# 32 bytes between the 128-feature chunks of the normed tokens and of the FFN's inner tiles

## The chip, the core and the metric

The kernel runs on one core of a Trainium2 chip. The metric is device time in microseconds for one execution of the whole program, the median of several runs. Lower is better.

## What is computed

256 tokens of 1024 features go through two transformer layers and then a third block. Each of the two layers is an FFN, an attention mixer with 16 heads, and another FFN; the third block has a recurrent mixer beside a latent attention, then a layer of 16,384 experts that are found by key products, and a last gated projection. Cut to the parts that the change touches:

```
def rms_norm(x, g):
    y = xf * lax.rsqrt(jnp.mean(xf * xf, axis=-1, keepdims=True) + RMS_EPS)
    return y * g

def swiglu(x, w_gate, w_up, w_down):
    return (jax.nn.silu(x @ w_gate) * (x @ w_up)) @ w_down

for layer in range(DEPTH):
    x = x + 0.5 * swiglu(rms_norm(x, norm_ffn1[layer]), ...)
    x = x + mixed(rms_norm(x, norm_mix[layer]) @ w_in ...) @ w_out[layer]
    x = x + 0.5 * swiglu(rms_norm(x, norm_ffn2[layer]), ...)
...
h = rmsnorm(x, g_mix);  u = h @ w_in              # 4384 columns
x = x + merged @ w_out
x = x + peer_ffn(rmsnorm(x, g_ffn), ...)          # gelu(h @ expert_u.T), gates, @ expert_v
x = x + (p @ w_ple_proj) * sigmoid(rmsnorm(x, g_ple) @ w_ple_gate)
```

All inputs are float32, and D_FF is 2816.

## The kernel before

Activations lie feature-major: a tile of 128 partitions has one chunk of 256 tokens for each 128 features, so `x`, `xnh` and `xnl` have KD = 8 chunks and the FFN's inner tiles `hh` and `hl` have KF = 22. A chunk is 256 float32 values, 1024 bytes of each partition.

Precision comes from splitting. Every value is kept as a high part in float32r and the rest in a second float32r tile (`xnh` and `xnl` for the normed tokens, `hh` and `hl` for the inner activations, `o0` and `o1` for the gated expert activations, `gh` and `gl` for the tokens of the key products, `yh` and `yl` for the mixers' outputs). A product takes three matmuls: high by high, low by high, high by low.

Nearly all work is streaming weights once. `wblk` (line 186) loads a block of four 128x128 weight tiles, 256 KB, by a DMA on SP's queue into `wr`, ScalarE makes the high part `wh` (line 195), and VectorE or GpSimd, as the stage says, makes the rest `wl` (line 201). Each of `wr`, `wh` and `wl` has 2048 bytes a partition and comes from the pool `wp` with four buffers, or, for every fifth block, from a second pool with one.

`ws` (line 213) then runs three matmuls for each of the four weight tiles, with the weights as the stationary operand and a 256-column chunk as the moving one:

```
self.nc.tensor.matmul(out, wh[:, s], h, start=first, stop=False, **kw)   # line 224
self.nc.tensor.matmul(out, wh[:, s], l, start=False, stop=False, **kw)   # line 225
self.nc.tensor.matmul(out, wl[:, s], h, start=False, stop=last, **kw)    # line 226
```

So a product with 8 chunks is two blocks and 24 matmuls. The stages, in order, are:

- `ffn` (line 282), four times: 22 x 2 products with `xnh` and `xnl` for gate and up, then 8 products of 22 chunks with `hh` and `hl` for down.
- `mix`, after the first FFN of each layer: 2 x 16 products with `xnh` and `xnl` as moving operand for queries and keys, 8 chunks x 2 x 2 x 3 matmuls for the values, where the tokens are the stationary operand and 512 weight columns move (lines 205 to 207), attention, and the output product with `yh` and `yl`. In the second layer `forget_gates` runs the same `xnh` and `xnl` chunks against weights of 8 columns (lines 159, 205 to 207).
- `mix2`: 35 products with `xnh` and `xnl`, the recurrence and the latent attention among them; `xnh` and `xnl` then hold other values for 96 and 192 more matmuls.
- `peer`: the key products with `gh` and `gl`, then 128 calls of `u_phase` (line 1237), one product with `xnh` and `xnl` each. 30 of them run while the key products' top 16 are sorted, with `wl` made by GpSimd; 34 in a loop that VectorE feeds with one-hot tiles (lines 1266 to 1285); 64 in turn with the first 64 of 128 calls of `v_phase` (line 1290), which stream `o0` and `o1` (lines 1302 to 1304).
- `ple`: the last gate, 8 products with `xnh` and `xnl`.

Tiles are placed in SBUF pool by pool, in the order in which they are made. Bytes from the partition's start, as the built program has them: `xnh` at 10,496 and `xnl` at 18,688, then the weight tiles from 26,880 on (`wh` of the first buffer at 35,072), `hh` at 65,824 and `hl` at 88,352, `o0`, `o1`, `gh`, `gl`, `yh` and `yl` behind 65,536. Every 128x128 weight tile starts at 256 modulo 512, whichever buffer it is in. Every chunk of `xnh` and `xnl` starts at 256, too; every chunk of `hh`, `hl`, `yh` and `yl` at 288, and of `o0`, `o1`, `gh` and `gl` at 320. "Offset" below is the start of the moving chunk less that of the weight tile, modulo 512: 0 for `xnh` and `xnl`, 32 for `hh`, `hl`, `yh` and `yl`, 64 for the others.

Of the kernel before, what the change touches and what calls it, by code (L numbers as in the profile page):

```python
# [10 lines left out]
F32R = mybir.dt.float32r  # L11
# [9 lines left out]
T = 256  # L21
D = 1024
KD = D // 128
FF = 2816
KF = FF // 128
# [117 lines left out]
class Prog:  # L143
    def __init__(self, ctx, tc, A):
        self.ctx, self.tc, self.nc, self.A = ctx, tc, tc.nc, A
        nc = self.nc
        self.const = ctx.enter_context(tc.tile_pool(name="const", bufs=1))
        self.table("natural_log_exp_and_others")
        self.vec = self.const.tile([128, N_VEC], F32, name="vec")
        nc.sync.dma_start(self.vec, A["vec"])  # L150
        self.ones = self.const.tile([128, 128], F32, name="ones")
        nc.vector.memset(self.ones, 1.0)
        self.eps = self.const.tile([128, 1], F32, name="eps")
        nc.vector.memset(self.eps, 1e-6)
        self.x = self.const.tile([128, KD, T], F32, name="x")
        self.xnh = self.const.tile([128, KD, T], F32R, name="xnh")
        self.xnl = self.const.tile([128, KD, T], F32R, name="xnl")

    def col(self, name, i=0):
        o, n = VEC_COLS[name]  # L160
# [121 lines left out]
    def ffn(self, gname, gu, dn, also=None):  # L282
        nc, tc = self.nc, self.tc
        self.norm(gname)
        with tc.tile_pool(name="hp", bufs=1) as hp:
            hh = hp.tile([128, KF, T], F32R, name="hh")
            hl = hp.tile([128, KF, T], F32R, name="hl")
            for f in range(KF):
                if f == 4 and also is not None:
                    also()  # L290
                p = self.pair("mm")
                for j in range(2):
                    self.ws(p[:, j], gu[f, j], self.xnh, self.xnl, KD)
                if f == 0:
                    self.norm_factor()
                s = self.tmp.tile([128, 2, T], F32, name="s")
                nc.vector.tensor_mul(s, p, self.rs2())
                nc.scalar.activation(s[:, 0], s[:, 0], AF.Silu)
                nc.vector.tensor_mul(s[:, 0], s[:, 0], s[:, 1])
                self.split(hh[:, f], hl[:, f], s[:, 0])  # L300
            for d in range(KD):
                p = self.pair("mm")
                self.ws(p[:, 0], dn[d], hh, hl, KF)
                nc.vector.scalar_tensor_tensor(self.x[:, d], p[:, 0], 0.5, self.x[:, d], op0=ALU.mult, op1=ALU.add)
# [1235 lines left out]
```

## Time and profile before

| | |
|---|---|
| median of 3 runs | 2279.07 us (2274.92 to 2279.41) |
| the profiled execution | 2276.94 us |
| its span | 2275.2 us |
| TensorE, matmuls | 2196.3 us busy, 97%, 18034 matmuls |
| TensorE, weight loads | 2114.0 us busy, 93% |
| VectorE | 1617.6 us, 71% |
| ScalarE | 1346.1 us, 59% |
| GpSimd | 283.0 us, 12% |
| HBM, mean over the span | 159 GB/s read and written |

The profiled execution lies 1.7 us above its own span, which is what stands before the first and after the last instruction, and 2.1 us under the median of the runs. Busy time is the union of an engine's records. Matmuls overlap in the records, so their mean duration is longer than the time from one to the next. Stages can be told by the tiles: a window of the trace in which only `xnh` and `xnl` are streamed is a gate and up projection, one with `hh` and `hl` a down projection.

### The profile page before, as it was taken

What the parts mean: (1) busy time and instruction counts of PE and PEld (TensorE: products, weight loads), DVE (VectorE), ACT (ScalarE), POOL (GpSimd) and SP (SyncE); (2) the same over time, 40 slices, a digit from 0 to 9 for tenths busy, and PEclk for the clock granted to TensorE, in tenths of its full rate; (3) what the DMA queues carried; (4) which work ended last, traced back from release to release, by engine and by line L of the source; (5) the groups of instructions that cost most, each with busy time, mean ns of one, the idle gap of its engine ahead of it and who ended that gap; (6) DMA issues with size and microseconds to landing.
All of it is one profiled execution on the core that took longest, in us unless ns stands there. A gap on an engine that the chain in (4) does not pass through costs nothing.

```text
span 2275.2 us, 48212 instructions
## 1 busy us (share of the span) xinstructions
PE 2196.3 (97%) x18034; PEld 2114.0 (93%) x18034; DVE 1617.6 (71%) x3293; ACT 1346.1 (59%) x2667; POOL 283.0 (12%) x272
## 2 busy tenths in 40 slices
PE   8999999999999999999888989889999999999997
PEld 8999889999999789999787889889999999999997
DVE  7766777666766757766886577999996666666666
ACT  6555576556555556556765656456665555555556
POOL 1001100000000101001233027960000000000001
PEclk9999999999999999999998999999999999999999
DMA  6566425565567325565243145443346555555553
GB/s 208 183 181 193 125 94 192 183 183 187 184 179 223 116 83 173 183 181 185 86 134 113 47 156 172 149 140 112 121 144 206 185 185 186 183 189 189 187 186 117
DMA packets 209659, 365.30 MB, mean 161 GB/s; under 512 B 31056, under 2 KB 39312, under 8 KB 208912
## 3 DMA queue, kind: packets, MB, share of 16 engines
q1 hardware_dynamic: 207312, 361.96, 50.4%
q8 instruction: 141, 2.31, 0.4%
q14 instruction: 94, 0.77, 0.1%
q10 hardware_dynamic: 2112, 0.26, 0.1%
HBM read 357.87 MB, written 4.26 MB: 159 GB/s over the span
## 4 chain that ended last, share of the span: by engine, by line
PE 82%; DVE 9%; ACT 3%; DMA 2%; POOL 2%; issue 2%; SPq 0%; DVEq 0%; POOLq 0%; ACTq 0%
PE mm L224 13%; PE mm L226 13%; PE mm L225 13%; PE acc L1302 5%; PE acc L1304 5%; PE acc L1303 5%; PE pu L225 5%; PE pu L224 5%; PE pu L226 5%; DVE wl L201 2%; PE pg L1282 2%; POOL wl L201 1%; DMA wr<-in_pu 1%; PE w L347 1%; PE mm L205 1%
## 5 line engine op out<-in xcount | busy, mean ns | idle before, releaser
L195 ACT ACTIVATE wh<-wr 128x512 fp32r<-128x512 f32 (+1 forms) x1348 | 836.4, 624 | 697.0 <-PE mm L225 240.5
L201 DVE TENSOR_TENSOR wl<-wr,wh 128x512 fp32r<-128x512 f32 (+1 forms) x1234 | 851.6, 696 | 485.5 <-ACT wh L195 455.7
L224 PE MATMUL mm<-xnh,wh 128*128 128x256 f32 x1840 | 529.2, 288 | 10.6 <-ACT wh L195 7.3
L226 PE MATMUL mm<-xnh,wl 128*128 128x256 f32 x1840 | 524.4, 285 | 1.6 <-POOL wl L201 0.9
L225 PE MATMUL mm<-xnl,wh 128*128 128x256 f32 x1808 | 514.7, 285 | 0.1
L224 PEld LDWEIGHTS mm<-xnh,wh 128*128 128x128 f32 x1840 | 355.0, 193 | 15.1 <-ACT wh L195 11.4
L226 PEld LDWEIGHTS mm<-xnh,wl 128*128 128x128 f32 x1840 | 355.0, 193 | 3.9 <-POOL wl L201 1.5
L225 PEld LDWEIGHTS mm<-xnl,wh 128*128 128x128 f32 x1808 | 349.1, 193 | 2.7 <-issue 1.9
L226 PE MATMUL pu<-xnh,wl 128*128 128x256 f32 x1024 | 291.2, 284 | 11.1 <-POOL wl L201 10.6
L224 PE MATMUL pu<-xnh,wh 128*128 128x256 f32 x1024 | 292.9, 286 | 0.0
L225 PE MATMUL pu<-xnl,wh 128*128 128x256 f32 x1024 | 289.6, 283 | 0.0
L1302 PE MATMUL acc<-o,wh 128*128 128x256 f32 x1024 | 286.9, 280 | 0.0
L1304 PE MATMUL acc<-o,wl 128*128 128x256 f32 x1024 | 285.8, 279 | 0.0
L1303 PE MATMUL acc<-o,wh 128*128 128x256 f32 x1024 | 285.7, 279 | 0.0
L226 PEld LDWEIGHTS pu<-xnh,wl 128*128 128x128 f32 x1024 | 195.6, 191 | 13.2 <-POOL wl L201 12.5
L226 PE MATMUL mm<-hh,wl 128*128 128x256 f32 x704 | 197.8, 281 | 0.0
L224 PE MATMUL mm<-hh,wh 128*128 128x256 f32 x704 | 197.1, 280 | 0.0
L224 PEld LDWEIGHTS pu<-xnh,wh 128*128 128x128 f32 x1024 | 196.0, 191 | 0.0
L225 PEld LDWEIGHTS pu<-xnl,wh 128*128 128x128 f32 x1024 | 195.8, 191 | 0.0
L225 PE MATMUL mm<-hl,wh 128*128 128x256 f32 x704 | 195.7, 278 | 0.0
L1304 PEld LDWEIGHTS acc<-o,wl 128*128 128x128 f32 x1024 | 192.4, 188 | 0.1
L1302 PEld LDWEIGHTS acc<-o,wh 128*128 128x128 f32 x1024 | 192.5, 188 | 0.0
(458 smaller groups left out, 3897.7 us busy)
## 6 DMA issues: line engine op xcount, KB each, us to landing
wr<-in_ffn_gu SPq DMA_DIRECT2D x352, 256.0 KB, 2.9
wr<-in_pu SPq DMA_DIRECT2D x256, 256.0 KB, 2.9
wr<-in_pv SPq DMA_DIRECT2D x256, 256.0 KB, 2.9
wr<-in_ffn_d SPq DMA_DIRECT2D x160, 256.0 KB, 2.8
wr<-in_qk SPq DMA_DIRECT2D x64, 256.0 KB, 3.0
wr<-in_wo SPq DMA_DIRECT2D x48, 256.0 KB, 2.9
wr<-in_v SPq DMA_DIRECT2D x32, 256.0 KB, 2.8
wr<-in_u_g SPq DMA_DIRECT2D x32, 256.0 KB, 2.7
```

The costliest lines, as they stand in the source:

```text
L195: nc.scalar.activation(wh[:, :n], wr[:, :n], AF.Copy)
L201: (self.nc.gpsimd if eng == "p" else self.nc.vector).tensor_sub(out, a, b)
L205: nc.tensor.matmul(out, lh, rh, start=start, stop=False)
L224: self.nc.tensor.matmul(out, wh[:, s], h, start=first, stop=False, **kw)
L225: self.nc.tensor.matmul(out, wh[:, s], l, start=False, stop=False, **kw)
L226: self.nc.tensor.matmul(out, wl[:, s], h, start=False, stop=last, **kw)
L347: nc.tensor.matmul(O[s, 0:T], vtok[:, 0, hv * 64:hv * 64 + 64], PT[:, 0:256], start=True, stop=False)
L1282: nc.tensor.matmul(pg[:, j], o[0][:, j], o[1][:, j], start=True, stop=True)
L1302: nc.tensor.matmul(o, vh[:, s], ph, start=first, stop=False, skip_group_check=True)
L1303: nc.tensor.matmul(o, vh[:, s], pl, start=False, stop=False, skip_group_check=True)
L1304: nc.tensor.matmul(o, vl[:, s], ph, start=False, stop=last, skip_group_check=True)
```

## The change

Four tiles get 8 more columns in each chunk, and the name is bound to a view without them. Nothing reads or writes the 32 bytes between.

```
-        self.xnh = self.const.tile([128, KD, T], F32R, name="xnh")
-        self.xnl = self.const.tile([128, KD, T], F32R, name="xnl")
+        self.xnh = self.const.tile([128, KD, T + 8], F32R, name="xnh")[:, :, :T]
+        self.xnl = self.const.tile([128, KD, T + 8], F32R, name="xnl")[:, :, :T]
...
-            hh = hp.tile([128, KF, T], F32R, name="hh")
-            hl = hp.tile([128, KF, T], F32R, name="hl")
+            hh = hp.tile([128, KF, T + 8], F32R, name="hh")[:, :, :T]
+            hl = hp.tile([128, KF, T + 8], F32R, name="hl")[:, :, :T]
```

The built programs have the same instructions in the same order on all five engines. The addresses differ: chunks are 1056 bytes apart instead of 1024. `xnh` stays at 10,496, `xnl` moves to 18,944, the weight tiles move up by 512 bytes (and so stay at 256 modulo 512), `hh` goes to 66,336 and `hl` to 89,568. Offsets to the weight tiles, modulo 512, for chunk k or f:

| tile | before | after |
|---|---|---|
| `xnh` | 0 | 32 k: 0 to 224 |
| `xnl` | 0 | 256 + 32 k: 256 to 480 |
| `hh` | 32 | 32 + 32 f: 0 in chunk 15 alone |
| `hl` | 32 | 224 + 32 f: 0 in chunk 9 alone |
| `yh`, `yl`; `o0`, `o1`, `gh`, `gl` | 32; 64 | 32; 64 |

## Rows read from the trace of the kernel before

**Rows 1.** The page's head: span, and busy time by engine.
```profile
span 2275.2 us, 48212 instructions
PE 2196.3 (97%) x18034; PEld 2114.0 (93%) x18034; DVE 1617.6 (71%) x3293; ACT 1346.1 (59%) x2667; POOL 283.0 (12%) x272
```

**Rows 2.** The page's chain that ended last, share of the span by line.
```profile
PE mm L224 13%; PE mm L226 13%; PE mm L225 13%; PE acc L1302 5%; PE acc L1304 5%; PE acc L1303 5%; PE pu L225 5%; PE pu L224 5%; PE pu L226 5%; DVE wl L201 2%; PE pg L1282 2%; POOL wl L201 1%; DMA wr<-in_pu 1%; PE w L347 1%; PE mm L205 1%
```

**Rows 3.** Windows, TensorE's matmuls: window, length, busy (count), clock, DMA share, GB/s.
```profile
30.00:130.00 100.00, 100.00 (x835) 1.00 0.60 190
140.00:200.00 60.00, 60.00 (x512) 1.00 0.66 186
350.00:450.00 100.00, 100.00 (x836) 1.00 0.57 183
470.00:520.00 50.00, 50.00 (x426) 1.00 0.65 186
2050.00:2150.00 100.00, 100.00 (x852) 1.00 0.58 187
```

**Rows 4.** Timeline of TensorE in a gate and a down projection: start, length in us.
```profile
400.03 0.28 PE L224 MATMUL mm<-xnh,wh 128*128 128x256 f32 x1
400.15 0.28 PE L225 MATMUL mm<-xnl,wh 128*128 128x256 f32 x1
400.27 0.28 PE L226 MATMUL mm<-xnh,wl 128*128 128x256 f32 x1
...
494.80 0.28 PE L226 MATMUL mm<-hh,wl 128*128 128x256 f32 x1
494.92 0.28 PE L224 MATMUL mm<-hh,wh 128*128 128x256 f32 x1
495.04 0.28 PE L225 MATMUL mm<-hl,wh 128*128 128x256 f32 x1
495.15 0.28 PE L226 MATMUL mm<-hh,wl 128*128 128x256 f32 x1
```

**Rows 5.** Timeline of TensorE in the forget gates, first and last of nine rows.
```profile
736.98 0.28 PE L205 MATMUL mm<-xnh,wfh 128*8 128x256 f32 x1
...
737.89 0.28 PE L207 MATMUL mm<-xnh,wfl 128*8 128x256 f32 x1
```

**Rows 6.** Windows, busy us (count) of PE, PEld, DVE, ACT, POOL; clock, DMA, GB/s.
```profile
740.00:850.00 110.00, 107.23 (x687) 87.54 (x686) 73.66 (x208) 65.06 (x157) 10.38 (x8) 1.00 0.31 98
...
1065.00:1335.00 270.00, 238.58 (x2275) 211.98 (x2274) 202.33 (x427) 184.93 (x433) 71.07 (x89) 0.94 0.32 98
...
1455.00:1515.00 60.00, 49.31 (x394) 47.40 (x393) 59.20 (x91) 26.89 (x51) 58.23 (x34) 1.00 0.43 140
1515.00:1680.00 165.00, 161.96 (x1363) 159.62 (x1363) 163.16 (x350) 102.72 (x172) 1.99 (x2) 1.00 0.36 117
1680.00:2040.00 360.00, 360.00 (x3026) 359.89 (x3026) 226.38 (x415) 196.23 (x381) 0.00 (x0) 1.00 0.58 187
...
2228.00:2275.00 47.00, 35.67 (x253) 32.81 (x252) 30.45 (x61) 30.13 (x64) 5.70 (x7) 0.90 0.36 118
```

**Rows 7.** TensorE's waits from 1300 to 1720 us: total us, times, longest.
```profile
PE pu L226 <- POOL wl L201: 10.9, 9, 1.6
```

**Rows 8.** Groups of ScalarE's line 174, which writes the high parts: busy, mean ns.
```profile
L174 ACT ACTIVATE o<-ga 128x256 fp32r<-128x256 f32 x128 | 51.4, 402 | 0.0
L174 ACT ACTIVATE hh<-s 128x256 fp32r<-128x256 f32 x88 | 35.5, 403 | 0.5 <-DVE s L299 0.5
...
L174 ACT ACTIVATE xnh<-xn 128x256 fp32r<-128x256 f32 x8 | 3.1, 412 | 5.0 <-DVE xn L1359 4.9
```

**Rows 9.** Timeline of TensorE where attention follows a projection, at 236 us.
```profile
236.04 0.29 PE L226 MATMUL mm<-xnh,wl 128*128 128x256 f32 x1
236.17 0.27 PE L341 MATMUL w<-c_ident,z 128*128 128x128 f32 x1
```

## The prediction, made before the change ran

> **What bounds the kernel now.** I read the shares by engine first, then the chain, then the pace of TensorE in stretches where it never stops, and last the stretches where it does stop.
>
> TensorE is busy 2196.3 of the 2275.2 us of the span [rows 1], and the chain that ended last is mostly its matmuls, with line 224 alone at 13% [rows 2]. So the time is close to the number of matmuls times the time from one start to the next, and that step is what to look at. A matmul lasts 0.28 us in the records, but the next starts long before it ends, so a duration says nothing of the pace. Counts in full windows do. In [rows 3] TensorE is busy through each window at full clock. A window counts every matmul that touches it, so I take off 2.4 (0.28 us divided by the 0.12 us step). The gate and up projections of the FFN, which stream `xnh` and `xnl`, then make 100 us / (836 - 2.4) = **120.0 ns** a matmul; the first window gives 120.1. The down projection, streaming `hh` and `hl`, makes 50 / (426 - 2.4) = 118.0 and, in the longer window, 60 / (512 - 2.4) = **117.7**; the expert values, streaming `o0` and `o1`, 100 / (852 - 2.4) = 117.7. I use 117.8 for these.
>
> These matmuls have the same shape: 128x128 weights, 256 columns, float32r. The single steps are in [rows 4]: with `xnh` 0.12 us without exception, with `hh` and `hl` 0.12, 0.12 and 0.11 in turn, because one of the three is shorter. The loop, the helper, the DMA size and the ACT and DVE work per block are alike, too. What differs is the address: `xnh` and `xnl` chunks begin at the weights' own address modulo 512 (offset 0), `hh` and `hl` 32 bytes on, `o0` and `o1` 64 bytes on.
>
> One more stretch tells whether the place of `xnh` is slow by itself. The forget gates stream the same `xnh` and `xnl` chunks against weights of 8 columns: from 736.98 to 737.89 us lie eight steps, so 0.91 / 8 = 0.114 us each [rows 5]. At the same addresses, with almost no weights to read, the stream runs faster than with `hh`. So the 120 ns holds a part that the weight load takes while the columns stream, and that part is 6 ns at offset 0 and 4 ns at the offsets 32 and 64.
>
> **The change, part by part.** No instruction is added, removed or moved; only addresses change. The four normed and inner tiles grow by 32 bytes a chunk, and the weight tiles move up by 512 bytes, which leaves them where they were modulo 512. Offsets of the moving chunk to the weights become 0, 32, ..., 224 for the eight chunks of `xnh`, 256, ..., 480 for those of `xnl`, and for `hh` and `hl` they run through all sixteen multiples of 32.
>
> What a matmul costs at an offset other than 0, 32 and 64 no stretch shows. The bounds are the longest and the shortest step that this stream has: 120.0 ns (no gain), and 113.7 ns, where the weight load almost vanishes. I take 117.8, the mean at both offsets that I have, since it does not differ between 32 and 64. That is a gain of 2.2 ns. Per block of 8 chunks 24 matmuls run, 16 of them with `xnh`; chunk 0 of `xnh` (2 of 24) stays at offset 0, so 22 of 24 gain. Stage by stage, with counts from the loops:
>
> - FFN, gate and up, four times: 4 x 22 x 2 x 24 = 4224 matmuls. TensorE never stops there [rows 3], so all of it counts: 4224 x 22/24 x 2.2 ns = 8.5 us.
> - Query and key projections, 2 x 16 x 24 = 768: 1.5 us. TensorE is busy 107.23 of 110 us in such a stretch [rows 6], so I count all. The 192 matmuls of the value projection have `xnh` and `xnl` as weights and 512 moving columns; bounded by 0 and 192 x 2.2 ns, I take 0.4 us.
> - Second mixer, 35 x 24 + 96 + 192 = 1128 matmuls: 2.3 us at most. TensorE is busy 238.58 of 270 us at a mean clock of 0.94 [rows 6]; the rest are waits for short chains elsewhere. Half of it, 1.1 us.
> - First 30 expert keys, 720 matmuls: up to 1.5 us. From 1455 to 1515 us GpSimd is busy 58.23 of 60 us making `wl` and TensorE only 49.31 [rows 6], with nine waits of 10.9 us in all for it [rows 7]: a faster TensorE waits longer there. I count 0.3 us, for the stretch before.
> - The next 34, 816 matmuls: up to 1.6 us. VectorE is busy 163.16 of 165 us there and sets the pace [rows 6]: 0.
> - The last 64, 1536 matmuls among the expert values: TensorE is busy 360.00 of 360 us [rows 6]. 1536 x 22/24 x 2.2 = 3.1 us.
> - The gate of the last stage, 192 matmuls: 0.4 us, of which I take 0.3, since only 35.67 of 47 us are busy [rows 6].
> - Down projections: `hh` and `hl` come to offset 0 in one chunk of 22 each, so 3 of 66 matmuls lose 2.2 ns, and of 2112 that is 0.2 us lost.
>
> Writing the padded tiles costs nothing that I can find: each write is still one run of 256 elements. The same ScalarE copy takes 412 ns into `xnh` at offset 0, 403 into `hh` at 32 and 402 into `o` at 64 [rows 8], so a shift is worth 10 ns at most either way; on some 64 + 88 writes that is 1.5 us of an engine that is idle for 40% of the span and sets no end in these stages. The faster matmuls ask for weights 1.8% sooner; the DMA engines move 183 GB/s in such a window, and 186 at the quicker pace of `hh` [rows 3], so that supply holds.
>
> Sum: 8.5 + 1.5 + 0.4 + 1.1 + 0.3 + 3.1 + 0.3 - 0.2 = 15.0 us. The profiled execution took 2276.94 us, 2.1 below the median of the runs (2279.07), and its lowest run is 2274.92. So 2276.94 - 15.0 = 2261.9; I say **2262.0**.
>
> **The rivals.**
>
> *No change.* The 2.2 ns belong to something other than the offset: `xnh` and `xnl` lie in the first 27 KB of a partition, beside the weight tiles, and `hh`, `hl`, `o0`, `o1` beyond 65 KB, so place and offset differ together in every row I have. If a place in the same part of the memory as the weights costs the 2.2 ns, nothing moves out of it, and the time stays at 2276.9. For it: the two cannot be told apart by [rows 3]. Against it: the extra is the same in every step [rows 4], as two reads in a fixed phase would make it, and not a scatter as from traffic of other engines. The Trainium skill speaks for this rival ("SBUF — State Buffer", section "SBUF: two separate sides"): TensorE, ScalarE and VectorE's own ports "never wait on anyone", and TensorE has a second read port for weights, so no address should matter. By that rule the sum is 0; the forget gates' steps, shorter by 6 ns once there is little weight to read, already disagree with it. Chance 0.16.
>
> *A shorter period.* If what clashes repeats every 128 bytes rather than 512, offsets 128, 256 and 384 are as bad as 0; 32 and 64 still are not. Then a quarter of the chunks stay at 120 ns: 15.2 x 0.75 / 0.917 = 12.4 us, less a quarter of 2112 matmuls x 2.2 ns = 1.2 us, so 11.2 us and 2265.7. Nothing in the trace excludes it. Chance 0.12.
>
> *Slower: the far half of the offsets.* From 256 to 480 the columns begin behind the weights' address and may run into them early. All of `xnl` lies there, so 8 of 24 matmuls, and of the down projection 29 of 66 (8 of 22 chunks of `hh`, twice each, and 13 of 22 of `hl`). Let each cost c above 120 ns. The near half (14 of 24) gains 9.7 us by the terms above; the far half costs 2.5 c in us, and the down projection 0.93 (c + 2.2). It turns to a loss from c = 2.2, that is 122.2 ns a matmul. The one step of an `xnh` stream before a weight load at offset 480 is 236.04 to 236.17, 0.13 us instead of 0.12 [rows 9], which speaks for it; but the next instruction there is of another kind, and its own start may be what is late. At twice that cost, 124.4 ns, it gives -9.7 + 11.0 + 6.1 = 7.4 us, so 2284. Chance 0.10.
>
> **How the numbers follow.** The flat gain has 0.62, the shorter period 0.12, no change 0.16, the far half 0.10. Faster, same and slower mean more or less than 0.2%, some 4.6 us, about what a measurement of this kernel can tell from no change. Faster takes the first two, 0.74; of the far half a little ends near zero, so same 0.17 and slower 0.09. The range goes down to 2250, where the unseen offsets gain 4 ns instead of 2.2 (15.2 x 4 / 2.2 = 27.6 us, under half of the way to the bound of 113.7), and up to 2279, which holds no change at the median of the runs. Left out are the far half as priced and gains near the lower bound. The likeliest case alone, with 117 to 118.6 ns at the new offsets, spans 2256 to 2268.
>
> **What would show it.** After the change, full windows of the gate and up projections should hold 850 matmuls in 100 us instead of 836, the down projection's still 426 in 50, and the expert values' still 852 in 100. The four FFNs should each be 2.1 us shorter, 1680 to 2040 us by 3, and the stretches that GpSimd and VectorE hold should stay as long as they are. Single steps should still read 0.12 for chunk 0 of `xnh` and be shorter for the others. If steps with `xnl` are longer than 120 ns, the far half is real; if all stay at 120, the offset was not the cause; if every fourth chunk stays at 120, the period is 128.

## The result, and the profile after

The changed kernel takes **2254.03 us** (median of 4 runs, 2252.64 to 2257.27), the kernel before 2279.24 (2274.92 to 2279.99): a ratio of 0.9895, with an interval from 0.9878 to 0.9912. That is 25 us less; the forecast of 2262.0 lay 17 under the median of the kernel before (its sum was 15.0 us, taken from a profiled execution 2.1 us under that median). The time lies in the range. The profiled execution took 2254.32 us, its span is 2252.5.

The page's head of the changed kernel, beside [rows 1]:

```profile
span 2252.5 us, 48212 instructions
PE 2169.9 (96%) x18034; PEld 2087.4 (93%) x18034; DVE 1619.1 (72%) x3293; ACT 1346.9 (60%) x2667; POOL 283.0 (13%) x272
```

TensorE is busy 26.4 us less with the same 18034 matmuls, and the other engines as long as before. So the matmuls follow each other faster. Where, the same windows as in [rows 3] tell, all at the same granted clock of 1.00 (window, length, busy with the count, clock, DMA share, GB/s):

```profile
30.00:130.00 100.00, 100.00 (x848) 1.00 0.60 193
140.00:200.00 60.00, 60.00 (x509) 1.00 0.65 186
350.00:450.00 100.00, 100.00 (x847) 1.00 0.58 186
470.00:520.00 50.00, 50.00 (x425) 1.00 0.63 184
2050.00:2150.00 100.00, 100.00 (x885) 1.00 0.60 194
```

The first and third line are the gate and up projections: 835 and 836 matmuls became 848 and 847, not the 850 of the forecast. The down projections got a little slower: 512 became 509, 426 became 425. The last line is the surprise. The expert values stream `o0` and `o1`, whose offset to the weights is 64 before and after, and they went from 852 to 885.

For the step I take the first and the last start of an unbroken stretch and divide by the steps between. This gives 120.2 ns before and 118.5 after for gate and up, 117.8 and 118.4 for down, and **117.8 and 113.3** for the expert values.

The same happens where keys and expert values take turns. First the window before, then after (columns as above):

```profile
1680.00:2020.00 340.00, 340.00 (x2858) 1.00 0.58 187
```

```profile
1680.00:2020.00 340.00, 339.38 (x2927) 1.00 0.59 193
```

And the timeline of TensorE in the changed kernel at a change from keys to values (start, length in us):

```profile
1723.04 0.28 PE L226 MATMUL pu<-xnh,wl 128*128 128x256 f32 x1
1723.16 0.28 PE L1302 MATMUL acc<-o,wh 128*128 128x256 f32 x1
1723.27 0.28 PE L1303 MATMUL acc<-o,wh 128*128 128x256 f32 x1
1723.39 0.28 PE L1304 MATMUL acc<-o,wl 128*128 128x256 f32 x1
...
1725.88 0.28 PE L224 MATMUL pu<-xnh,wh 128*128 128x256 f32 x1
```

From the first value matmul (1723.16) to the next key matmul (1725.88) lie 24 steps, so 2.72 / 24 = 0.1133 us each.

Stage by stage, from the starts of the stages in the two traces:

| stretch (before) | before | after | shorter by | forecast |
|---|---|---|---|---|
| four FFNs, gate and up | | | 7.0 | 8.5 |
| four FFNs, down | | | -1.3 | -0.2 |
| two mixers of the layers, 201 to 346 and 719 to 871 us | 296.6 | 297.9 | -1.3 | 1.9 |
| second mixer, 1056 to 1334 us | 277.4 | 274.2 | 3.2 | 1.1 |
| from there to the first 30 keys, 1334 to 1419 us | 85.7 | 84.0 | 1.7 | 0 |
| the first 30 keys, 1419 to 1513 us | 93.7 | 91.3 | 2.4 | 0.3 |
| the loop of 34 keys, 1513 to 1684 us | 170.4 | 176.0 | -5.6 | 0 |
| keys and values in turn, 1684 to 2044 us | 360.0 | 351.6 | 8.4 | 3.1 |
| values alone, 2044 to 2227 us | 183.6 | 176.6 | 7.0 | 0 |
| the rest | | | 1.2 | 0.3 |
| span | 2275.2 | 2252.5 | 22.7 | 15.0 |

The two lines with values hold 15.4 of the 22.7 us. About 13.6 of it is the values' own step: 3072 matmuls at 4.4 ns each.

Some of the other lines are in part the clock's and not the step's. The granted clock has two levels, 1.00 (2.4 GHz) and 0.50 (1.2 GHz), and for a few microseconds here and there it stands at the lower one. Where it does so differs between the two profiles. In the second mixer (`mix2`), the same stretch of work before and after:

```profile
1098.80:1108.60 9.80, 9.80 (x34) 0.50 0.09 27
```

```profile
1094.00:1100.50 6.50, 6.50 (x39) 1.00 0.12 40
```

That is worth some 4 us, more than the 3.2 of its line. Two kernels of the next section whose `xnh` and `xnl` keep their offsets (512 bytes of place, and the padding for `hh` and `hl` only) take 273.2 and 273.1 us for this stage instead of 277.4, so the 3.2 are not shown to be the change's. The 1.7 of the line below are such a stretch, too: the kernel before has the lower clock for a part of this window, and the changed one has 1.00 in all of it.

```profile
1380.00:1400.00 20.00, 18.14 (x141) 0.91 0.45 145
```

And in the first layer's mixer it is the changed kernel that runs slowly for a while, after TensorE has waited 2.2 us for `x`; the kernel before waits 2.1 us there and stays at 1.00:

```profile
338.20:341.40 3.20, 3.20 (x18) 0.50 0.56 180
```

One step got longer with the change. In the layers' value projections `xnh` and `xnl` are the weights, and 512 columns of `wh` or `wl` move. Six steps of it, before and after:

```profile
209.63 0.39 PE L205 MATMUL mm<-wh,xnh 128*128 128x512 f32 x1
...
210.99 0.39 PE L205 MATMUL mm<-wh,xnh 128*128 128x512 f32 x1
```

```profile
209.62 0.39 PE L207 MATMUL mm<-wh,xnl 128*128 128x512 f32 x1
...
211.02 0.40 PE L207 MATMUL mm<-wh,xnl 128*128 128x512 f32 x1
```

That is 1.36 / 6 = 0.227 us before and 1.40 / 6 = 0.233 after. Over a whole stretch it is 227.4 and 232.7 ns.

The loop of 34 keys did not itself get longer. These are its own matmuls, before and then after (line, count, min/median/max ns, first to last start):

```profile
L1282 PE MATMUL pg<-o,o x512: 270/275/348, 1521.1 to 1680.5; 128*128 128x128 f32 x171
```

```profile
L1282 PE MATMUL pg<-o,o x512: 270/275/348, 1515.5 to 1674.5; 128*128 128x128 f32 x171
```

That is 159.4 and 159.0 us. The 5.6 us were lost at its front. TensorE's waits of the changed kernel from 1295 to 1715 us (total us, times, longest), beside [rows 7]:

```profile
PE pu L226 <- POOL wl L201: 9.1, 8, 1.6
PE pg L1414 <- DVE res L1409: 4.3, 1, 4.3
```

The first 30 keys now end 11.7 us sooner in the program, and GpSimd holds them 1.8 us less, but VectorE's sort of the top 16 is not done by then. Its last instruction, which writes `res`, starts at 1512.3 us before and at 1505.3 after, only 7.0 us sooner. So TensorE has a wait of 4.3 us for `res`, which the kernel before did not have. Behind this wait comes a stretch at the lower clock, which takes its share (the kernel before has 1.00 from 1513 to 1521 us):

```profile
1505.60:1512.20 6.60, 5.97 (x28) 0.50 0.39 122
```

The loop can begin only 5.6 us sooner.

### The profile page after: what moved, and what is told of

Its sections match the earlier page's. It is cut to its first block, busy times and chain, and to the rows that moved or that the text cites. A ratio compares the mean times of both kernels' runs of the same rounds, so it can differ in the third digit from the quotient of the medians.

```text
span 2252.5 us, 48212 instructions
## 1 busy us (share of the span) xinstructions
PE 2169.9 (96%) x18034; PEld 2087.4 (93%) x18034; DVE 1619.1 (72%) x3293; ACT 1346.9 (60%) x2667; POOL 283.0 (13%) x272
## 4 chain that ended last, share of the span: by engine, by line
PE 80%; DVE 14%; ACT 3%; DMA 2%; issue 1%; POOL 1%; SPq 0%; DVEq 0%; ACTq 0%; POOLq 0%
PE mm L224 13%; PE mm L225 13%; PE mm L226 13%; PE acc L1304 5%; PE acc L1302 5%; PE acc L1303 5%; PE pu L225 4%; PE pu L224 4%; PE pu L226 4%; DVE wl L201 2%; PE pg L1282 2%; PE w L347 1%; PE mm L205 1%; DVE o L1278 1%; PE mm L207 1%
## 5 line engine op out<-in xcount | busy, mean ns | idle before, releaser
L224 PEld LDWEIGHTS mm<-xnh,wh 128*128 128x128 f32 x1840 | 349.2, 190 | 16.7 <-ACT wh L195 12.7
L226 PEld LDWEIGHTS mm<-xnh,wl 128*128 128x128 f32 x1840 | 349.2, 190 | 5.0 <-POOL wl L201 2.4
L225 PEld LDWEIGHTS mm<-xnl,wh 128*128 128x128 f32 x1808 | 343.7, 190 | 2.4 <-issue 1.9
L1302 PE MATMUL acc<-o,wh 128*128 128x256 f32 x1024 | 282.7, 276 | 0.4 <-ACT wh L195 0.4
L1303 PE MATMUL acc<-o,wh 128*128 128x256 f32 x1024 | 282.6, 276 | 0.0
```

The source lines that it names most:

```text
L1302: nc.tensor.matmul(o, vh[:, s], ph, start=first, stop=False, skip_group_check=True)
L1303: nc.tensor.matmul(o, vh[:, s], pl, start=False, stop=False, skip_group_check=True)
```

## The experiments

Two questions were open. Is it the offset or the place of the tiles that sets the step? And how can the expert values, whose chunks keep their offset, become faster? The first theory said offset: each matmul's step depends on its own offset alone. The second said place: where the tiles lie in the partition. A third came with the result: the step depends on the offset and also on something that the stream before leaves behind. Below, "step" is always the mean from start to start, read from the one profiled execution of each kernel; the times are of all its runs.

### The place alone

An unused tile of 512 bytes behind `xnl` puts the weight tiles and everything behind them 512 bytes up, near where the change puts them, with every offset as before.

```
+        self.const.tile([128, 128], F32, name="gap")     # behind xnl
```

> The kernel before, with an unused 512-byte tile behind xnl, so that all later tiles stand where the change puts them, while every offset between chunks and weights stays as it was. After the change the expert values alone ran at 113.3 ns a matmul instead of 117.8, though their own offset of 64 did not change. Theory of place (the pace of a stream hangs on where its tiles lie): expert values at 113.3 ns here too, some 13 us faster, about 2265 us. Theory of a carried state (a stream of one constant offset has two paces, and the stream before it decides which): nothing changes, xnh at 120.0, hh at 117.8, expert values at 117.8, time within 0.2% of before.

Measured: 2278.41 us (10 runs) beside 2277.41, ratio 1.0011 (1.0001 to 1.0021). The steps stay at 120.2, 117.8 and 117.8 ns. Gate and up, and the expert values (columns as above):

```profile
30.00:130.00 100.00, 100.00 (x836) 1.00 0.64 192
...
2060.00:2160.00 100.00, 100.00 (x851) 1.00 0.65 187
```

So the values are not faster because `o0`, `o1` or the weights moved. The place falls, as far as 512 bytes of it can tell.

### One half of the change each

The padding for `xnh` and `xnl` only:

```
+        self.xnh = self.const.tile([128, KD, T + 8], F32R, name="xnh")[:, :, :T]
+        self.xnl = self.const.tile([128, KD, T + 8], F32R, name="xnl")[:, :, :T]
```

> Only xnh and xnl get the 32 bytes; hh and hl keep 1024-byte chunks at offset 32. Both theories: gate and up projections at 118.5 ns as after the change, the down projections back at 117.8 instead of 118.4, 1.3 us less than the change, about 2253 us. Carried state: the expert values at 113.3, as after the change, since the u_phase streams before them are the same. If the hh chunks had a part in that pace, they would go back to 117.8 and the time to 2266.

Measured: 2253.0 us, ratio 0.9888 (0.9872 to 0.9905). Its windows in a down projection, a gate and up projection and the expert values:

```profile
145.00:195.00 50.00, 50.00 (x431) 1.00 0.67 190
350.00:450.00 100.00, 100.00 (x847) 1.00 0.65 187
...
2060.00:2160.00 100.00, 100.00 (x885) 1.00 0.67 195
```

All of the gain is here. The 847 matmuls are those of the change. The values run at 885, with only `xnh` and `xnl` padded (up to 2182 us; what happens there stands in the last section). And the down projection went from 427 in 50 us (the run with 512 bytes) to 431, 116.7 ns a step, though `hh` and `hl` keep their offset of 32. Two streams that the edit does not touch became faster.

The padding for `hh` and `hl` only:

```
+            hh = hp.tile([128, KF, T + 8], F32R, name="hh")[:, :, :T]
+            hl = hp.tile([128, KF, T + 8], F32R, name="hl")[:, :, :T]
```

> Only hh and hl get the 32 bytes; xnh, xnl and all weights stay. Both theories: down projections at 118.4 instead of 117.8, 1.3 us more, about 2280 us, which may not show against noise; gate and up at 120.0, expert values at 117.8.

Measured: 2277.01 us, ratio 1.0 (0.999 to 1.0009); down at 118.4 ns, gate and up and the values as before. This half of the change is worth nothing that shows.

### One constant offset

`xnh` and `xnl` at a constant offset of 64, by unused tiles of 64 and 448 bytes ahead of and behind them.

```
+        self.const.tile([128, 16], F32, name="gap0")      # ahead of xnh
+        self.const.tile([128, 112], F32, name="gap1")     # behind xnl
```

> Chunks of xnh and xnl stay 1024 bytes apart, but both tiles begin 64 bytes on against the weights, so every chunk has the constant offset 64 that o0 and o1 have. Theory of the offset alone: gate and up projections at 117.8 ns or better for all chunks, 16 us faster, about 2262 us. Theory of two paces: such a constant stream runs at 117.8 or at 113.3 ns throughout; at 113.3 the FFN stages alone give 28 us and the expert values 13 more, about 2230 us. Theory that xnh is slow because it lies beside the weight tiles: still 120.0 ns, about 2277 us.

Measured: 2261.39 us (5 runs, 2243.06 to 2262.67), ratio 0.991 (0.9876 to 0.9945); gate and up at 118.0 ns, the values at 117.8. Two of its down projections, the third and the fourth FFN's:

```profile
655.00:705.00 50.00, 50.00 (x431) 1.00 0.66 187
990.00:1040.00 50.00, 50.00 (x419) 1.00 0.65 184
```

The same tiles, the same addresses, the same loop: 116.7 ns a step in one and 120.0 in the other. No theory of addresses alone can say that. The runs of this kernel lie 20 us apart, too, which those of the other kernels do not, except for one below.

### What passes from stream to stream

If the keys' stream leaves something behind that the values go on with, its last chunk is the first suspect. Here only chunk 7 is moved, to offsets 224 and 480, where the change has it; chunks 0 to 6 stay at 0. A small class `Chunks` holds a tile with the chunks at listed starts (in bytes).

```
+        self.xnh = Chunks.make(self.const, "xnh", 8448, [0, 1024, 2048, 3072, 4096, 5120, 6144, 7392])
+        self.xnl = Chunks.make(self.const, "xnl", 8960, [256, 1280, 2304, 3328, 4352, 5376, 6400, 7904])
```

> Chunks 0 to 6 of xnh and xnl keep offset 0 as before the change; only chunk 7 stands where the change puts it (offset 224 and 480). Theory of a carried state: the stream that follows takes over the phase that chunk 7 leaves, so the expert values run at 113.3 ns as after the change, and the time falls by some 13 us to about 2264, while gate and up projections stay near 120 ns in 21 of 24 matmuls. Theory that the gain comes from all chunks standing apart: the expert values stay at 117.8, gate and up gain an eighth of 1.6 ns, about 2276 us.

Measured: 2271.58 us, ratio 0.9977 (0.9965 to 0.9989); gate and up at 119.4 ns, down at 116.7, values still at 117.8. The last chunk alone does not do it for the values. It does for the down projection.

The other way round: the chunks as in the run with `xnh` and `xnl` only, but chunk 7 back at offset 0.

```
+        self.xnh = Chunks.make(self.const, "xnh", 8704, [0, 1056, 2112, 3168, 4224, 5280, 6336, 7680])
+        self.xnl = Chunks.make(self.const, "xnl", 8704, [256, 1312, 2368, 3424, 4480, 5536, 6592, 7680])
```

> The change to xnh and xnl alone, but chunk 7 of both back at offset 0. Carried state: the expert values fall back to 117.8 ns and the time goes up by 12 us against the variant with xnh and xnl alone, to about 2265, while the gate and up projections stay near 118.5. Theory that all chunks count: a loss of an eighth of the gain, about 2256 us, the expert values still at 113.3.

Measured: 2262.66 us, ratio 0.9939 (0.9918 to 0.996). Gate and up and the expert values:

```profile
350.00:450.00 100.00, 100.00 (x851) 1.00 0.60 187
...
2060.00:2160.00 100.00, 100.00 (x851) 1.00 0.60 187
```

Gate and up are even quicker than in the run with all chunks padded (851 to 847), although the offset of one chunk in eight went to the slowest step; the steps of single offsets do not simply add. But the values are back at 851, and the kernel is 10 us slower. So in the padded layout the values lose the quick step when chunk 7 goes back to 0, and chunk 7 alone, in the run before this one, does not bring it.

### Sixteen offsets in one run

For each product the weights are put further on in a larger buffer, so that the offset is constant within a product and goes through a list: in the FFNs, and in the values alone, where each offset holds for 96 matmuls. To make room, a pool of the expert stage has 22 buffers instead of 26.

```
-        wh = pool.tile([128, self.wk * 128], F32R, name="wh")
+        wh = pool.tile([128, self.wk * 128 + 128], F32R, name="wh")[:, o:o + self.wk * 128]
...
+                    self.shift = -self.SCAN[self.nffn][f] % 512
```

> Offsets measured by themselves: the buffers of wh and wl get 512 spare bytes, and each block of weights starts as far into its buffer as gives the wanted offset to the moving chunks. In the gate and up projections each of 22 steps (48 matmuls) has one constant offset: all 16 multiples of 32 rising, then falling, then multiples of 16, then in a mixed order; each of the 8 down products of an FFN has one; and the last 64 calls for the expert values, which never stop, take every multiple of 32 for 4 calls (96 matmuls). To make room, 22 instead of 26 buffers hold expert activations, so the total time is no comparison. Theory of the offset alone: one pace per offset, the same in every stage and order, 120.0 at 0. Theory of a carried state: at one offset different paces (113.3, 116.7, 117.8, 120.0) by what ran before, and the fast pace never at offset 0.

One run, 2278.75 us. The timeline of TensorE in the values alone, the first matmul at offset 32, 64, 96, 128, 160, 192, 224, 256, 288 and 320 in turn:

```profile
2057.80 0.28 PE L1302 MATMUL acc<-o,wh 128*128 128x256 f32 x1
...
2069.00 0.28 PE L1302 MATMUL acc<-o,wh 128*128 128x256 f32 x1
...
2080.31 0.28 PE L1302 MATMUL acc<-o,wh 128*128 128x256 f32 x1
...
2091.83 0.28 PE L1302 MATMUL acc<-o,wh 128*128 128x256 f32 x1
...
2103.22 0.28 PE L1302 MATMUL acc<-o,wh 128*128 128x256 f32 x1
...
2114.48 0.28 PE L1302 MATMUL acc<-o,wh 128*128 128x256 f32 x1
...
2125.79 0.28 PE L1302 MATMUL acc<-o,wh 128*128 128x256 f32 x1
...
2137.14 0.28 PE L1302 MATMUL acc<-o,wh 128*128 128x256 f32 x1
...
2148.65 0.28 PE L1302 MATMUL acc<-o,wh 128*128 128x256 f32 x1
...
2159.85 0.28 PE L1302 MATMUL acc<-o,wh 128*128 128x256 f32 x1
```

Each difference divided by 96 gives the step:

| offset | 32 | 64 | 96 | 128 | 160 | 192 | 224 | 256 | 288 |
|---|---|---|---|---|---|---|---|---|---|
| us | 11.20 | 11.31 | 11.52 | 11.39 | 11.26 | 11.31 | 11.35 | 11.51 | 11.20 |
| ns a step | 116.7 | 117.8 | 120.0 | 118.6 | 117.3 | 117.8 | 118.2 | 119.9 | 116.7 |

From 288 on the row repeats, up to 480 (118.3). So the offset counts, and its period is **256 bytes**, with 120 ns at 0 and at 96. It is the difference of the two addresses that counts, and not the place of the moving chunk: in this run offset 96 takes 119.9 to 120.1 ns with `xnh`, `hh` and `o0` alike, whose chunks start at 256, 288 and 320 modulo 512. The mean over one period is 118.3, and the padded tiles, whose chunks walk through just these offsets, measure 118.5 (`xnh`) and 118.4 (`hh`).

But one offset need not have one step. Twice in the first FFN the weights stand at offset 64. These are the first matmuls of the first such product and of the product behind it, then the same for the second:

```profile
24.39 0.28 PE L224 MATMUL mm<-xnh,wh 128*128 128x256 f32 x1
...
29.84 0.28 PE L224 MATMUL mm<-xnh,wh 128*128 128x256 f32 x1
...
114.72 0.28 PE L224 MATMUL mm<-xnh,wh 128*128 128x256 f32 x1
...
120.38 0.28 PE L224 MATMUL mm<-xnh,wh 128*128 128x256 f32 x1
```

Each stretch has 48 steps: 5.45 / 48 = 113.5 ns the first time, 5.66 / 48 = 117.9 the second. Ahead of both stands a product at offset 32. Over the whole run, the offsets 64, 192, 320 and 448 settle at either 113.3 or 117.8. The offset 32 shows 116.7 or 117.8, two of the three steps that the down projection had above without a change of its own (the third is 120.0, in the run with one constant offset). At 160 and 416 it is 117.3 or 118.7, and once 120.0. At 0 and 256 the step always settles at 120.0.

### Attempts to bring about the quick step

Four layouts were meant to combine offset 64 with what leaves the quick step behind. The first has chunks 0 to 6 at 64 and chunk 7 at 224 and 480.

```
+        self.xnh = Chunks.make(self.const, "xnh", 8448, [64, 1088, 2112, 3136, 4160, 5184, 6208, 7392])
+        self.xnl = Chunks.make(self.const, "xnl", 8960, [320, 1344, 2368, 3392, 4416, 5440, 6464, 7904])
```

> Chunks 0 to 6 of xnh and xnl at the constant offset 64, chunk 7 at 224 and 480 as after the change; hh and hl at offset 32. Carried state: after chunk 7 a stream at offset 64 starts in the phase of 113.3 ns, as the expert values do after the change, so gate, up and u_phase products run at 113.3 ns for 21 of 24 matmuls, some 114 in the mean, and the expert values at 113.3: about 24 us in the FFNs, 13 in the expert values and some 10 in u_phase, about 2230 us. If phase does not carry over, 118 ns and about 2260 us.

Measured: 2261.87 us, ratio 0.9927 (0.9902 to 0.9952), values at 117.8: a miss.

The second does the same for `hh` and `hl`, with chunk 21 moved.

```
+            hh = Chunks.make(hp, "hh", 22720, [32 + 1024 * f for f in range(21)] + [21696])
+            hl = Chunks.make(hp, "hl", 23296, [352 + 1024 * f for f in range(21)] + [22272])
```

> As the variant before (xnh and xnl at offset 64 with chunk 7 at 224 and 480), and also hh and hl at offset 64 with chunk 21 at 224 and 480. Carried state: the down projections, too, run at 113.3 ns for 63 of 66 matmuls, 9 us less for the four, about 2221 us. If phase does not carry over, no difference from the variant before.

Measured: 2258.49 us (8 runs, 2241.96 to 2268.56), ratio 0.9907 (0.9876 to 0.9938). Gate and up in the second FFN and in the fourth, and down in the fourth:

```profile
350.00:450.00 100.00, 100.00 (x850) 1.00 0.59 186
880.00:980.00 100.00, 100.00 (x881) 1.00 0.64 194
...
990.00:1040.00 50.00, 50.00 (x443) 1.00 0.65 188
```

With one layout three FFNs run at 118 and the fourth at 114. Its runs lie 27 us apart.

The third has chunk 0 at 0 and all others at 64, for all four tiles; the fourth steps by 128 bytes from chunk to chunk, from 64 on.

```
+        self.xnh = Chunks.make(self.const, "xnh", 8256, [0, 1088, 2112, 3136, 4160, 5184, 6208, 7232])
```

```
+        self.xnh = Chunks.make(self.const, "xnh", 9152, [64, 1216, 2368, 3520, 4672, 5824, 6976, 8128])
```

> xnh, xnl, hh and hl: chunk 0 at offset 0, all others at 64. In the scan a stream that had run at offset 0 went on at 113.3 ns at offset 64 in four of four changes inside the FFNs, but at 117.8 in the expert values. Carried state, with offset 0 always setting the same phase: every product runs chunk 0 near 120 and the rest at 113.3, 114.2 in the mean, about 2225 us. If three matmuls at offset 0 do not set the phase, products stay at 118 and the time near 2260, with runs that differ from one another.

> xnh, xnl, hh and hl: chunk k at offset 64 + 128 k modulo 512, so always 64 or 192 modulo 256, the two places where the scan found 113.3 or 117.8 ns; the scan also showed equal paces for offsets 256 apart. In the scan three steps among these offsets that began at 113.3 stayed there, and one of 64 to 448 went from 117.8 to 113.3. Carried state, with each step of 128 pushing towards the fast phase: products at 113.3 to 114 throughout, expert values at 113.3 after them, about 2220 us. If the step changes nothing: 117.8 ns, about 2260 us.

Measured: 2269.0 us, ratio 0.9958 (0.9941 to 0.9975), and 2261.06, ratio 0.993 (0.9912 to 0.9948). Both keep the values at 117.8, and their own streams between 117.8 and 118.8: two more misses. I have no rule for which of the two steps a layout falls into.

### The best of what was seen

The run with `xnh` and `xnl` alone had the values at 113.3, at a constant 64. So `hh` and `hl` are put at a constant 64 as well, by 32 unused bytes ahead of `hh`; their chunks are not padded.

```
+        self.xnh = self.const.tile([128, KD, T + 8], F32R, name="xnh")[:, :, :T]
+        self.xnl = self.const.tile([128, KD, T + 8], F32R, name="xnl")[:, :, :T]
...
+            hp.tile([128, 8], F32, name="gap")      # ahead of hh
```

> The change to xnh and xnl alone, and hh and hl moved up by 32 bytes, so that all their chunks keep one offset, 64 instead of 32. After the change to xnh and xnl the expert values, at offset 64, ran at 113.3 ns in all 63 calls that follow a u_phase. Carried state: the last chunks of the up projection leave the same phase, so the four down projections run at 113.3 ns instead of 116.7, 528 x 3.4 ns = 1.8 us each, 7 us in all, about 2246 us; everything else as in the variant with xnh and xnl alone. If the phase at the end of the up projection is another one than in u_phase, or does not carry over to hh, 117.8 ns and 2.4 us more, about 2255 us.

Measured: **2247.59 us** (4 runs, 2244.63 to 2249.61), ratio 0.9857 (0.9835 to 0.9879), beside 0.9895 for the change. Down in the first and second FFN, and the values:

```profile
145.00:195.00 50.00, 50.00 (x443) 1.00 0.69 196
...
470.00:520.00 50.00, 50.00 (x444) 1.00 0.68 194
2060.00:2160.00 100.00, 100.00 (x885) 1.00 0.66 194
```

All four down projections run at 113.3 ns, and at 1042 us the kernel is 9.8 us ahead of the changed one. 5.8 of them are gone by 1406 us, 3.5 in the second mixer and 2.2 behind it. In both the granted clock stands at 0.50 for a while where the changed kernel has 1.00 for the same work: 21 matmuls from 1084.8 to 1091.4 us and 16 from 1371.6 to 1374.6.

## Why the prediction was right, and where it was wrong

**The step is what to look at: right.** TensorE has the same number of matmuls and is busy 26.4 us less.

**The offset matters, the place does not: right.** With 512 bytes of place and no change of offset the ratio is 1.0011. The rival *No change* falls: an offset modulo 256 moves the step between 113.3 and 120.0 ns here. The rule of the Trainium skill that stood behind it ("SBUF — State Buffer", section "SBUF: two separate sides") says that TensorE's port and some others "never wait on anyone", where engines contend for ports. No run here tests that; what falls is the conclusion drawn from it, that no address matters.

**2.2 ns at every other offset: wrong as a rule, near in size.** The step that failed is "I take 117.8 [...] since it does not differ between 32 and 64". The two offsets I had happen to lie near the mean. Over the period the steps go from 116.7 to 120.0 in the values alone, and offset 96 is as bad as 0. Walking through all of them gives about their mean, so gate and up gained 1.7 ns and 7.0 us, not 8.5. By the same mean the down projection, which stood better than the mean, lost 1.3 us instead of 0.2. The bound of 113.7, read from the forget gates as the step with almost no weight load, is none: at offset 64 full weight loads ran at 113.3. So the 6 and 4 ns that the prediction gave to the weight load are not shown to be its price.

**The expert values still 852 in 100 us: wrong, and the largest miss.** The sum had 0 for them because their chunks don't move, and 3.1 for the stretch in turn. They gained 7.0 there alone and about 6.7 of the 8.4 in turn. The runs show that this comes through `xnh` and `xnl` (padding these alone gives 885, moving tiles by 512 bytes gives 851), and that it needs chunk 7 off offset 0 (851 without). What it is that passes from one stream to the next the records don't show. That the sum came out near is therefore partly luck: without the values' own 13.6 us the gain would have been some 9.

**The layers' mixers, 1.9 us: wrong.** They got 1.3 us longer. I took a gain of 0.4 for the 192 matmuls of the value projections, because they use the same tiles. There the term failed: with `xnh` and `xnl` as weights, the offset 0 had the shorter step, and they lost 5.3 ns each, 1.0 us in all. The queries and keys did gain, some 0.5 us a layer, so the two cancel: in the second layer's mixer the time from 719 to 871 us is the same before and after, 151.7 us. The 1.3 us are the stretch at a granted clock of 0.50 in the first layer's mixer. From 201 to 346 us the six kernels without such a stretch there take 144.6 to 145.0 us, the eight with one 145.7 to 146.8.

**The second mixer (`mix2`), 1.1 us: not shown.** It got 3.2 us shorter, but the granted clock accounts for that much, and two kernels with the old offsets of `xnh` and `xnl` are as short.

**The first 30 keys and the loop, 0.3 and 0: right for the loop, and short of a wait.** The loop that VectorE feeds stayed at 159 us. In the 30 keys TensorE did not wait longer for GpSimd, as the prediction had it, but 1.8 us less. But I did not name what is late next when TensorE arrives sooner: VectorE's sort, now a wait of 4.3 us. With the lower clock behind it, it costs 5.6 us: the keys' gain and part of what was gained ahead of them.

**The rivals.** *A shorter period* was half right: the period is 256, not 512, and not 128 (128 and 384 are at 118.6 to 118.8, not at 120). *Slower: the far half* falls: in the values alone 288 and 32 take 116.7 both, 480 and 224 take 118.3 and 118.2.

## What to carry to other kernels

Where one engine is the bound, compare the start-to-start step of instructions of one shape between stages: a stage that is 2% slower for no reason of its own is a lead, and here it led to where the moving chunks and the weights lie modulo 256 bytes. Try several layouts on the chip, with the streams that the edit does not touch in view; here more than half of the gain came from one of those. And take a layout whose runs lie far apart, as at a constant 64 for `xnh`, for one whose step can fall either way. Before a stage is credited with a gain, read its granted clock in both profiles: one stretch of 10 us at 0.50 made a mixer 4 us longer here, with no part of the change in it.

## What the runs showed of the hardware that was not expected

- Matmuls of one shape (128x128 float32r weights, 256 columns) at full granted clock settled at steps between 113.3 and 120.0 ns here, by the offset between moving chunk and weights modulo 256 bytes. Offset 96 costs as much as 0.
- With `xnh` and `xnl` as the weights and 512 columns moving, it is the other way round: 227.4 ns with all chunks at offset 0 (also with 512 bytes of place), 232.7 with the padded chunks and 233 at the constant 64.
- At 64 and 192, and 256 bytes on, there are two settled steps, 113.3 and 117.8 ns; at 32 and 160, and 256 bytes on, there is more than one as well. Which one holds can differ between two products of one run at the same offset (113.5 and 117.9 ns), and in the changed kernel it is kept for a whole stretch of 1560 matmuls. There, too, while keys and values take turns, 63 of 64 calls of the values run at 113.3; the one at 1705.8 us, whose first steps are 0.23 and 0.50 us because weights came late, runs at 118. In the kernel before it is the other way round: 63 at 118, and at 113 the one at 1712.0 us, behind two long steps of 0.19 and 0.22 us. So an interruption can turn the step over, and it need not be long. In the run with `xnh` and `xnl` only, the values alone run at 113.3 ns up to one step of 0.14 us in their midst and at 117.8 behind it, to the end (start, length in us):

```profile
2182.17 0.28 PE L1302 MATMUL acc<-o,wh 128*128 128x256 f32 x1
2182.28 0.30 PE L1303 MATMUL acc<-o,wh 128*128 128x256 f32 x1
2182.42 0.28 PE L1304 MATMUL acc<-o,wl 128*128 128x256 f32 x1
```

Not every interruption does it: in the run with `hh` and `hl` at 64, the values' call at 1699.2 us has a step of 0.50 us and goes on at 113.3. Whether a pause put in on purpose would turn the step was not tried, and what inside the chip holds the state stays open.
